# A two-layer DiT block on one Trainium2 core: two modulation parts moved out of the first stage, two rows computed during routing

## The chip, the cores and the metric

One core of a Trainium2 chip. The time is that of one execution on the device in microseconds (us), the median of several runs. The engines are PE (TensorE, matmuls; PEld is its loading of stationary operands), DVE (VectorE), ACT (ScalarE), POOL (GpSimd) and SP (SyncE, which here only issues transfers).

## What is computed

```python
for layer in range(2):                                   # x 1024x1024, ctx 256x1024, all f32
    sh1, sc1, gt1, sh2, sc2, gt2 = split(silu(c) @ w_mod[layer] + b_mod[layer], 6)
    csh1, csc1 = the same from c_ctx, for layer 0's hc = rmsnorm(ctx) * (1 + csc1) + csh1
    hx = rmsnorm(x, norm_mix_g[layer]) * (1 + sc1) + sh1
    yx = mixer_ab(hx, hc) if layer == 0 else mixer_chunk_gmlp(hx)
    x = x + gt1 * yx
    h = rmsnorm(x, norm_ffn_g[layer]) * (1 + sc2) + sh2
    aff = softmax(h @ w_router); gate, idx = top_k(aff.T, 128)      # 16 experts, 128 rows each
    xe = h[idx]
    ye = ((silu(xe @ w_gate) * (xe @ w_up)) @ w_down) * gate
    x = x + gt2 * scatter_add(ye, idx)
return rmsnorm(x, final_norm_g)
```

`mixer_ab` (layer 0) is a bidirectional mLSTM of 4 heads beside a window attention of 8 heads, both with the context; `mixer_chunk_gmlp` (layer 1) a gated MLP in chunks of 128 rows.

## The kernel before

Each modulation vector is a *part* (layer, w), w from 0 to 5 in the order sh1, sc1, gt1, sh2, sc2, gt2: 1024 columns of `w_mod`, 4 MB. PE computes a part in eight steps `mod_step` (line 661), one for each 128 rows of `w_mod`, of four matmuls each, in four column groups of the array, with `silu(c)` stationary. The stationary operand is 32 columns wide; it comes from `silw`, a tile of copies of `silu(c)` and `silu(c_ctx)` that is built once and lies in the pool `mcol` of layer 0.

Large products are made of three: weights and activations are split in two (`mh` + `ml`, `xH` + `xL`, both fp32r), ACT making the high part, DVE (POOL for some) the low one, and PE multiplies high by high, high by low and low by high.

The stages, in order:

- **First stage** (`start`). `start_mod` computes parts (0,0) and (0,1) for x and ctx, with 8 MB that SP loads. Then `heads_context` goes through the four mLSTM heads of the context: each loads two `w_in` tiles of 512 KB (ring `wraw`, two buffers, line 78 issues on SP), splits them (lines 70 and 71) and projects (line 302); between them it takes pieces of two generators, `rows()`, which normalises and transposes x, and `mods`, the parts (0,2) and (0,3) by `mod_part` (line 682), whose 16 tiles of 512 KB POOL loads (line 688) into the buffers of x rows.
- **Mixer of layer 0** (`layer0_a`, `layer0_b`). A generator of modulation parts, (0,4), (0,5), (1,0), (1,1), (1,2) and (1,5), gives one step between every few pieces of the attention (line 617). A row of kind gt1 or gt2 is written to DRAM (`s_gt`), since it is later read along the free axis by all partitions; the others are turned to columns in `modc`. `layer0_b` ends with row stores `s_x`, `s_xr`, and loads by `hole_load` (line 703) the parts (1,3) and (1,4) into eight tiles of the experts' ring (`moe_tile`, 1 MB each, line 709, on SP).
- **Routing of layer 0.** `hole_mods` (line 712) multiplies these two parts while DVE sorts. The sort (lines 1030 to 1071) finds each expert's 128 rows, PE transposes (lines 1057 to 1101) thresholds, totals and lists, and POOL gathers the rows of expert 0 by an indirect transfer (`fetch(0)`). The first weights (`moe_open`) are split meanwhile (line 1161).
- **Experts** (`experts`). For each: gathered rows transposed (`xe`), high and low parts `xH`, `xL`; 24 tiles of weights split on ACT (`mh`) and DVE (`ml`); products `g`, `u` and `d` on PE (line 1175), `sg` the gated activation, `xe<-d` the scaling by gate and gt2 row, a scatter by POOL. Of the ring, tiles of the numbers in `HELD` are issued by POOL behind the first gather, all others by SP, each as soon as its buffer is free. The gt2 row is read from `s_gt` at the start.
- **Layer 1**: `mixer_chunk_gmlp`, its routing, its experts in the same way; its routing has no modulation work.

A scheduler orders each engine's instructions at build time from the order in the code and from its own estimate of times; where it interleaves the loops differently the code does not show it.

Of the kernel before, what the change touches and what calls it, by code (L numbers as in the profile page):

```python
# [8 lines left out]
F32 = mybir.dt.float32  # L9
# [3 lines left out]
AF = mybir.ActivationFunctionType  # L13
ALU = mybir.AluOpType
# [7 lines left out]
KD = 8  # L22
# [16 lines left out]
class Kernel:  # L39
# [142 lines left out]
    def start(self, rings):  # L182
        nc, I = self.nc, self.I
        with ExitStack() as late:
# [32 lines left out]
            pm = self.pool(late, "pmod0", space=PSUM)  # L217
            mods = itertools.chain(*(self.mod_part(xp, "xt", sm, pm, pt, 0, w) for w in (2, 3)))
            self.heads_context(late, pt, Ws, rows(), mods)

    def heads_context(self, s, pt, Ws, more, mods):
# [15 lines left out]
        for hd in range(4):  # L237
            W = Ws.pop(0) if Ws else self.w_in(512 + hd * 128)
            acc = self.pa.tile([128, 512], F32, tag="acc", name="acc")
            self.proj(acc[:, :NCTX], W, hc, 0, NCTX)  # L240
            pad = cpool.tile([128, NCTX + 4], F32, tag="cpad", name="cpad")
            nc.vector.memset(pad[:, 0:2], 0.0)
            nc.vector.memset(pad[:, NCTX + 2:NCTX + 4], 0.0)
            nc.scalar.activation(pad[:, 2:2 + NCTX], acc[:, :NCTX], AF.Copy)
            kc = cpool.tile([128, NCTX], F32, tag="kcT", name="kcT")
            self.conv_silu(pad, NCTX, 4 + hd, kc)
            list(itertools.islice(more, 2))
            list(itertools.islice(mods, (1, 1, 3, 3)[hd]))
            W = Ws.pop(0) if Ws else self.w_in(1024 + hd * 128)
            acc = self.pa.tile([128, 512], F32, tag="acc", name="acc")  # L250
            self.proj(acc[:, :NCTX], W, hc, 0, NCTX)
            vc = cpool.tile([128, NCTX], F32, tag="vcT", name="vcT")
            nc.scalar.activation(vc, acc[:, :NCTX], AF.Copy)
            if kept:
                store(*kept)
            kept = hd, kc, vc
            list(itertools.islice(more, 2))
            list(itertools.islice(mods, (0, 2, 3, 3)[hd]))
        store(*kept)
        for _ in itertools.chain(more, mods):  # L260
            pass
# [292 lines left out]
    def layer0_a(self, rings):  # L554
        nc, I = self.nc, self.I
        with ExitStack() as s:
# [60 lines left out]
            mods = itertools.chain(*(self.mod_part(lm, "wm", lm, pa, pt, i // 6, i % 6) for i in range(4, 12) if (i // 6, i % 6) not in self.HOLE))  # L617
# [44 lines left out]
    def mod_step(self, acc, k, wm):  # L662

        for j in range(4):
            self.nc.tensor.matmul(acc[32 * j:32 * j + 32, :], self.silw[:, k].rearrange("p a s -> p (a s)"), wm[:, 256 * j:256 * (j + 1)],  # L665
                                  start=(k == 0), stop=(k == KD - 1))
# [36 lines left out]
    def hole_load(self):  # L703

        self.hole = []
        for layer, w in self.HOLE:
            for kp in range(4):
                raw = self.moe_tile()
                self.nc.sync.dma_start(out=raw, in_=self.I["w_mod"][layer, 256 * kp:256 * (kp + 1), D * w:D * (w + 1)].rearrange("(k p) c -> p k c", p=128))
                self.hole.append(raw)  # L710

    def hole_mods(self, p, ps, pt):

        for i, (layer, w) in enumerate(self.HOLE):
# [7 lines left out]
            self.nc.gpsimd.tensor_tensor(m, m, self.bcols[:, 48 * layer + 8 * w:48 * layer + 8 * w + 8], op=ALU.add)  # L722

# [125 lines left out]
    def layer0_b(self, l0):  # L849
# [8 lines left out]
        with ExitStack() as s:  # L858
# [44 lines left out]
            self.hole_load()  # L903
# [273 lines left out]
    def experts(self, layer):  # L1177
        nc, I = self.nc, self.I
        with ExitStack() as s:
# [7 lines left out]
            nc.scalar.dma_start(out=gt2, in_=row_ap(self.s_gt, (2 * layer + 1) * D, D))  # L1187
# [177 lines left out]
            with self.tc.issue_after(self.listed):  # L1365
                self.first = [self.moe_low(*w) for w in self.first]
            gather(0)
            self.lists(p, pp, layer, groups.pop(0))
            fetch(1)
            self.lists(p, pp, layer, groups.pop(0))  # L1370
# [233 lines left out]
    def run(self):  # L1604
        nc = self.nc
        with ExitStack() as es:
# [52 lines left out]
            self.moe_open(self.m0, 0, 5)  # L1659
            with ExitStack() as r:  # L1660
# [13 lines left out]
            with ExitStack() as l1:  # L1674
# [7 lines left out]
                self.moe_open(self.m1, 1, 11)  # L1682
                self.moe_rings(self.m1, 1)
# [60 lines left out]
```

## Time and profile before

| | |
|---|---|
| median of 3 runs | 2697.33 us (2695.96 to 2702.22) |
| the profiled execution | 2693.89 us, span 2692.1 us |
| mean granted clock of PE | 0.967 of full speed |
| busy PE / PEld / DVE | 2495.9 / 1972.3 / 1891.8 us |
| busy ACT / POOL | 1508.6 / 610.6 us |
| transfers | 643.70 MB, mean 239 GB/s |
| first stage | 0 to 120 us |
| routing of layer 0 | 787 to 829 us |
| experts of layer 0, first `g` product | from 829.28 us |
| routing of layer 1 | 2050 to 2085 us |
| experts of layer 1, first `g` product | from 2084.75 us |

Busy times are of the profiled execution, and engines work side by side, so they do not add up to the span. Times in the rows below are us from the start of that span.

### The profile page before, as it was taken

Reading aid. Unit: us, or ns where it says so; the run is one execution under the profiler, and the core shown is the slowest. Engines: PE = TensorE matmul, PEld = TensorE weight load, DVE = VectorE, ACT = ScalarE, POOL = GpSimd, SP = SyncE. Lnnn points to the kernel's source line nnn. Section 1 sums busy time; section 2 is a strip of 40 time slices with the busy share of each in tenths; the row PEclk is TensorE's granted clock in tenths of the full one; section 3 lists DMA queues with packets and bytes.
Section 4 is the critical chain, followed back from the end, with each engine's and each line's share of the span. In section 5 each row is a group of like instructions: output and inputs, shape, how many; then the busy total and the mean of one; then the engine's idle time right before and its main releaser. Section 6 shows DMA issues by size and latency. Waiting matters only on the chain.

```text
span 2692.1 us, 34493 instructions
## 1 busy us (share of the span) xinstructions
PE 2495.9 (93%) x12543; PEld 1972.3 (73%) x12543; DVE 1891.8 (70%) x2826; ACT 1508.6 (56%) x2262; POOL 610.6 (23%) x399
## 2 busy tenths in 40 slices
PE   5899999978987999999998999999994999999996
PEld 3667777767765888887776887888883788888774
DVE  4568768668548999998884373216405899999887
ACT  4345444444245888887864233322323888888774
POOL 0100100035401122121003434443451022221101
PEclk8899999999988999999999999999996999999998
DMA  8543434284369999999956323342326999999995
GB/s 293 181 110 112 128 122 139 90 278 154 134 237 350 373 387 392 387 379 368 361 166 194 86 75 117 128 136 71 126 77 228 373 373 387 380 379 385 357 364 186
DMA packets 241223, 643.70 MB, mean 239 GB/s; under 512 B 18257, under 2 KB 84989, under 8 KB 240029
## 3 DMA queue, kind: packets, MB, share of 16 engines
q1 hardware_dynamic: 206768, 536.81, 53.4%
q0 software_dynamic: 23792, 83.43, 10.9%
q10 hardware_dynamic: 10492, 21.26, 2.4%
q8 instruction: 98, 1.61, 0.2%
q14 instruction: 73, 0.59, 0.1%
HBM read 588.79 MB, written 50.02 MB: 237 GB/s over the span
## 4 chain that ended last, share of the span: by engine, by line
PE 78%; DVE 9%; issue 4%; DMA 4%; ACT 3%; POOL 1%; POOLq 0%; ACTq 0%; DVEq 0%; SPq 0%
PE g L1175 13%; PE u L1175 13%; PE d L1175 12%; PE acc L302 7%; PE acc L1485 7%; PE acc L1559 6%; PE acc L1507 6%; PE acc L841 2%; PE S L495 1%; DMA wm<-in_w_mod_dram 1%; DMA wraw<-in_ab_w_in_dram 1%; PE acc L665 1%; PE tr L1205 1%; PE tr L1249 1%; DVE s2k L1501 1%
## 5 line engine op out<-in xcount | busy, mean ns | idle before, releaser
L71 DVE TENSOR_TENSOR ml<-mraw,mh 128x1024 fp32r<-128x1024 f32 x750 | 874.6, 1222 | 62.1 <-ACT mh L70 61.6
L70 ACT ACTIVATE mh<-mraw 128x1024 fp32r<-128x1024 f32 x750 | 767.1, 1063 | 129.7 <-PE g L1175 62.6
L71 POOL TENSOR_TENSOR wl<-wraw,wh 128x1024 fp32r<-128x1024 f32 (+1 forms) x132 | 257.2, 1958 | 346.7 <-ACT wh L70 346.7
L70 ACT ACTIVATE wh<-wraw 128x1024 fp32r<-128x1024 f32 (+1 forms) x163 | 143.1, 893 | 323.8 <-issue 123.6
L1175 PE MATMUL g<-mh,xH 128*128 128x512 f32 x512 | 206.2, 403 | 1.4 <-ACT xH L1210 1.4
L1175 PE MATMUL g<-ml,xH 128*128 128x512 f32 x512 | 205.7, 402 | 1.9 <-DVE ml L71 1.9
L1193 POOL DMA_INDIRECT xe<-s_xr,idx x32 | 148.3, 4634 | 256.4 <-ACT mh L70 125.7
L1175 PE MATMUL g<-mh,xL 128*128 128x512 f32 x512 | 204.3, 399 | 0.0
L1175 PE MATMUL u<-ml,xH 128*128 128x512 f32 x512 | 203.7, 398 | 0.2
L1175 PE MATMUL d<-ml,hidH 128*128 128x512 f32 x496 | 197.6, 398 | 5.9 <-DVE ml L71 5.9
L1175 PE MATMUL u<-mh,xH 128*128 128x512 f32 x512 | 202.2, 395 | 0.0
L1175 PE MATMUL u<-mh,xL 128*128 128x512 f32 x512 | 202.2, 395 | 0.0
L1273 POOL DMA_INDIRECT s_x<-xe,idx x28 | 45.1, 1612 | 683.0 <-ACT hidH L1251 446.8
L1175 PE MATMUL d<-mh,hidH 128*128 128x512 f32 x496 | 198.1, 399 | 1.6 <-DVE o L1270 1.6
L1175 PE MATMUL d<-mh,hidL 128*128 128x512 f32 x496 | 196.3, 396 | 0.0
L1485 PE MATMUL acc<-wh,h2k 128*128 128x512 f32 x512 | 163.7, 400 | 1.2 <-DVE h2k L1467 1.2
L1507 PE MATMUL acc<-h2k,wh 128*128 128x512 f32 x512 | 160.2, 394 | 0.0
L302 PE MATMUL acc<-hH,wh 128*128 128x512 f32 (+1 forms) x368 | 150.3, 409 | 3.2 <-ACT hx L533 1.2
L1559 PE MATMUL acc<-wh,s2k 128*128 128x512 f32 x480 | 152.1, 397 | 0.0
L302 PE MATMUL acc<-hH,wl 128*128 128x512 f32 (+1 forms) x368 | 145.1, 394 | 0.0
L302 PE MATMUL acc<-hL,wh 128*128 128x512 f32 (+1 forms) x368 | 145.0, 394 | 0.0
L688 POOL DMA_DIRECT2D wm<-in_w_mod_dram x64 | 34.6, 543 | 442.3 <-PE acc L665 388.9
(474 smaller groups left out, 5182.5 us busy)
## 6 DMA issues: line engine op xcount, KB each, us to landing
mraw<-in_moe_w_down_dram SPq DMA_DIRECT2D x128, 1024.0 KB
mraw<-in_moe_w_gate_dram SPq DMA_DIRECT2D x125, 1024.0 KB
mraw<-in_moe_w_up_dram SPq DMA_DIRECT2D x123, 1024.0 KB
wm<-in_w_mod_dram POOLq DMA_DIRECT2D x64, 512.0 KB, 4.5
wraw<-in_gm_w_in_dram SPq DMA_DIRECT2D x64, 512.0 KB
wraw<-in_gm_w_out_dram SPq DMA_DIRECT2D x32, 512.0 KB
wraw<-in_ab_w_in_dram SPq DMA_DIRECT2D x30, 512.0 KB
wm<-in_w_mod_dram SPq DMA_DIRECT2D x8, 1024.0 KB
```

Of the source, the lines that this page charges most:

```text
L70: nc.scalar.activation(h, src, AF.Copy)
L71: i = (nc.gpsimd if eng == "pool" else nc.vector).tensor_tensor(l, src, h.bitcast(F32), op=ALU.subtract)
L302: nc.tensor.matmul(acc, a[:, k, :], b[:, k, c0:c0 + n], start=(k == 0 and i == 0), stop=(k == KD - 1 and i == 2))
L495: nc.tensor.transpose(S[i][:, 512 - nl + j * 128:640 - nl + j * 128], P[:, j * 128:(j + 1) * 128], self.ident)
L688: nc.gpsimd.dma_start(out=wm, in_=self.I["w_mod"][layer, k * 128:(k + 1) * 128, D * w:D * (w + 1)])
L841: nc.tensor.matmul(acc, a[:, k, t * 128:(t + 1) * 128], b[:, k % 2, :], start=(k == 0 and i == 0), stop=(k == 3 and i == 2))
L1175: nc.tensor.matmul(acc[:, sl], a[:, k, :], b[:, sl], start=(k == 0 and i == 0), stop=(k == KD - 1 and i == 2))
L1193: f = nc.gpsimd.indirect_dma_start(out=xe, out_offset=None, in_=self.s_xr[layer], in_offset=bass.IndirectOffsetOnAxis(ap=self.idx[e], axis=0))
L1273: nc.gpsimd.indirect_dma_start(out=self.s_x[layer], out_offset=bass.IndirectOffsetOnAxis(ap=self.idx[e], axis=0), in_=o, in_offset=None, c ...
L1485: nc.tensor.matmul(acc[t], a[k][:, ts], b[:, k2, :], start=(k == 0 and i == 0), stop=(k == KD - 1 and i == 2))
L1507: nc.tensor.matmul(acc, a[:, k, :], b[k], start=(k == 0 and i == 0), stop=(k == KD - 1 and i == 2))
L1559: nc.tensor.matmul(acc, a[:, ts], b[k2], start=(c == 0 and i == 0), stop=(c == 15 and i == 2))
```

## The change

- Parts (0,2) and (0,3) are no longer in the first stage but in the generator of layer 0's mixer; the gate rows of the experts' outputs, parts (0,5) and (1,5), leave that generator.
- Each gate row is now computed in `experts`, by the new `hole_gate`, right after `fetch(0)` and ahead of `gather(0)` in the code. Its weights are four ring tiles: for layer 0 two loaded at the end of `hole_load`, two behind the first five weight tiles of `moe_open`; for layer 1 four behind `moe_open`. The accumulator is a `d` tile of PSUM, the bias comes by an ACT transfer, POOL adds it, ACT issues the write to `s_gt`. The read of the row moves behind `fetch(1)`.
- `mod_step` takes as its stationary operand one column of `sil`, read 32 times (stride 0), in place of the copies in `silw`.
- As the ring holds four more tiles of `w_mod` in each layer (12 in place of 8 before layer 0's experts), the numbers in `HELD` now meet other weight tiles.

```diff
     def start(self, rings):
...
-            pm = self.pool(late, "pmod0", space=PSUM)
-            mods = itertools.chain(*(self.mod_part(xp, "xt", sm, pm, pt, 0, w) for w in (2, 3)))
-            self.heads_context(late, pt, Ws, rows(), mods)
+            self.heads_context(late, pt, Ws, rows())
-    def heads_context(self, s, pt, Ws, more, mods):
+    def heads_context(self, s, pt, Ws, more):
-            list(itertools.islice(mods, (1, 1, 3, 3)[hd]))
...
-            list(itertools.islice(mods, (0, 2, 3, 3)[hd]))
...
...
-            mods = itertools.chain(*(self.mod_part(lm, "wm", lm, pa, pt, i // 6, i % 6) for i in range(4, 12) if (i // 6, i % 6) not in self.HOLE))
+            mods = itertools.chain(*(self.mod_part(lm, "wm", lm, pa, pt, i // 6, i % 6) for i in (2, 3, 4, 6, 7, 8)))
     def mod_step(self, acc, k, wm):
-            self.nc.tensor.matmul(acc[32 * j:32 * j + 32, :], self.silw[:, k].rearrange("p a s -> p (a s)"), wm[:, 256 * j:256 * (j + 1)],
+            self.nc.tensor.matmul(acc[32 * j:32 * j + 32, :], self.sil[:, k:k + 1].to_broadcast([128, 32]), wm[:, 256 * j:256 * (j + 1)],
...
+    def hole_gate(self, p, pd, layer):
+        nc, b = self.nc, self.I["b_mod"]
+        t = p.tile([128, D], F32, tag="sg", name="mrows")
+        rows, bias = t[:, 0:256], t[:, 256:512]
+        nc.scalar.dma_start(out=bias, in_=bass.AP(tensor=b.tensor, offset=b.offset + D * (6 * layer + 5), ap=[[256, 4], [0, 32], [1, 256]]))
+        acc = pd.tile([128, D], F32, tag="d", name="d")[:, 0:256]
+        for k in range(KD):
+            self.mod_step(acc, k, self.hole[k // 2][:, k % 2, :])
+        self.hole = []
+        nc.scalar.activation(rows, acc, AF.Copy)
+        nc.gpsimd.tensor_tensor(rows, rows, bias, op=ALU.add)
+        nc.scalar.dma_start(out=self.s_gt[2 * layer + 1].rearrange("(j c) -> j c", j=4), in_=rows[0:128:32, :])
...
-            self.hole_load()
+            self.hole = []
+            self.hole_load(self.HOLE)
+            self.hole_load([(0, 5)], range(2))
...
-            nc.scalar.dma_start(out=gt2, in_=row_ap(self.s_gt, (2 * layer + 1) * D, D))
...
             fetch(0)
...
+            self.hole_gate(p, pd, layer)
             gather(0)
             self.lists(p, pp, layer, groups.pop(0))
             fetch(1)
+            nc.scalar.dma_start(out=gt2, in_=row_ap(self.s_gt, (2 * layer + 1) * D, D))
...
             self.moe_open(self.m0, 0, 5)
+            self.hole_load([(0, 5)], range(2, 4))
...
                 self.moe_open(self.m1, 1, 11)
+                self.hole_load([(1, 5)])
```

How the built programs' instructions stand, at three places. First, DVE at the start of layer 0's sort, with what each instruction waits for (`work` is the sort's input, `sort` its result), before and then with the change:

```order
L1013 COPY rows<-tr 128x128 [waits PE_49]
L1014 COPY work<-rows 128x128 [waits DVE_49]
L1030 MAX sort_7116<-work 128x8 [waits DMASW3_49,DMASW1_49,DMASW5_49,DVE_49,PE_49]
L1030 MAX sort_7116<-work 128x8
L1033 MATCH_REPLACE work<-sort_7116,work 128x64 [waits DVE_49] x2
```
```order
L1025 COPY rows<-tr 128x128 [waits PE_49]
L1026 COPY work<-rows 128x128 [waits DVE_49]
L1042 MAX sort_7012<-work 128x8 [waits DMASW5_49,DMASW7_49,DMASW1_49,DVE_49]
L1042 MAX sort_7012<-work 128x8
L1045 MATCH_REPLACE work<-sort_7012,work 128x64 [waits DVE_49] x2
```
The first `MAX` has lost its wait on PE. On PE, at the same place, the routing transposes `tr` follow the two modulation parts `mod`, before and then with the change (`d<-mraw,sil` is the gate row):

```order
L665 MATMUL mod<-mraw,silw 32x256 x64
L677 MATMUL tr<-cst,mrows 128x128 x4
L1094 LDWEIGHTS zerob
L1094 MATMUL tr<-zerob 128x32
L1057 MATMUL tr<-sort_7115,cst 16x128
L1062 MATMUL tr<-thr,cst 128x1
L1076 MATMUL tr<-tot,cst 128x2
L1077 MATMUL tr<-tot,cst 128x2
L1085 MATMUL tr<-cst,gt 128x128
```
```order
L661 MATMUL mod<-mraw,sil 32x256 x29
L673 MATMUL tr<-cst,mrows 128x128 x2
L1106 LDWEIGHTS zerob
L1106 MATMUL tr<-zerob 128x32
L661 MATMUL d<-mraw,sil 32x256 x16
L1069 MATMUL tr<-sort_7011,cst 16x128
L1074 MATMUL tr<-thr,cst 128x1
L661 MATMUL d<-mraw,sil 32x256 x5
L1088 MATMUL tr<-tot,cst 128x2
L1089 MATMUL tr<-tot,cst 128x2
L661 MATMUL d<-mraw,sil 32x256 x3
L1097 MATMUL tr<-cst,gt 128x128
L661 MATMUL d<-mraw,sil 32x256 x5
```
The gate row's 32 matmuls go ahead of and between the routing transposes; the last of them stand behind the transposes of `gt` and of the lists, ahead of those of `xe`. Second, ACT from the splits of the first weights (`mh`, lines 1161 and 1173) to the first expert, before and then with the change:

```order
L1161 ACTIVATE mh<-mraw 128x1024 x4
L719 ACTIVATE mrows<-mod 128x256 x2
L720 ACTIVATE modc<-tr 128x8 x2
L1161 ACTIVATE mh<-mraw 128x1024
L1187 DMA gt_7328<-s_gt 128x1024
L1207 ACTIVATE xe<-tr,modc,gs_6484 128x128 x5
L1210 ACTIVATE xH<-xe 128x512
L1207 ACTIVATE xe<-tr,modc,gs_6484 128x128 x3
L1210 ACTIVATE xH<-xe 128x512
L70 ACTIVATE mh<-mraw 128x1024 x8
```
```order
L712 DMA mrows<-in_b_mod_dram 128x1x256
L717 ACTIVATE mrows<-d 128x256
L1173 ACTIVATE mh<-mraw 128x1024 x2
L719 DMA s_gt<-mrows 4x256
L1218 ACTIVATE xe<-tr,modc,gs_6376 128x128
L1173 ACTIVATE mh<-mraw 128x1024 x2
L1218 ACTIVATE xe<-tr,modc,gs_6376 128x128 x4
L1173 ACTIVATE mh<-mraw 128x1024
L1221 ACTIVATE xH<-xe 128x512
L1218 ACTIVATE xe<-tr,modc,gs_6376 128x128 x3
L1382 DMA gt_7224<-s_gt 128x1024
L1221 ACTIVATE xH<-xe 128x512
L70 ACTIVATE mh<-mraw 128x1024 x8
```
Five splits that stood ahead of the modulation copies and of the gather's evictions `xe` now stand behind the gate row's copy, three of them between the evictions. Third, DVE in layer 1 after `sg` of expert 10, up to the next `sg`, before and then with the change:

```order
L1230 TENSOR_TENSOR sg<-u,sg 128x512 x2
L71 TENSOR_TENSOR ml<-mraw,mh 128x1024
L1211 TENSOR_TENSOR xL<-xe,xH 128x512
L71 TENSOR_TENSOR ml<-mraw,mh 128x1024
L1211 TENSOR_TENSOR xL<-xe,xH 128x512
L71 TENSOR_TENSOR ml<-mraw,mh 128x1024 x5
L1270 SCALAR_TENSOR_TENSOR xe<-d,gate,gt_17208 128x512 x2
L71 TENSOR_TENSOR ml<-mraw,mh 128x1024
L1252 TENSOR_TENSOR hidL<-tr,hidH 128x512 x2
L71 TENSOR_TENSOR ml<-mraw,mh 128x1024 x14
```
```order
L1241 TENSOR_TENSOR sg<-u,sg 128x512 x2
L1222 TENSOR_TENSOR xL<-xe,xH 128x512 x2
L71 TENSOR_TENSOR ml<-mraw,mh 128x1024 x9
L1281 SCALAR_TENSOR_TENSOR xe<-d,gate,gt_17150 128x512 x2
L1263 TENSOR_TENSOR hidL<-tr,hidH 128x512 x2
L71 TENSOR_TENSOR ml<-mraw,mh 128x1024 x15
```
The two `xL`, which stood apart among the splits `ml`, stand together ahead of nine splits.

## Rows read from the trace of the kernel before

**Rows 1.** The page, part 4: shares of the chain that ended last, by engine.

```profile
PE 78%; DVE 9%; issue 4%; DMA 4%; ACT 3%; POOL 1%; POOLq 0%; ACTq 0%; DVEq 0%; SPq 0%
```

**Rows 2.** Windows, first stage: us, busy by engine (records), PEclk, DMA share, GB/s.

```profile
20.00:40.00 20.00, 11.91 (x78) 3.32 (x71) 5.17 (x13) 1.06 (x1) 1.10 (x2) 0.78 0.97 332
40.00:60.00 20.00, 15.39 (x96) 11.87 (x94) 15.95 (x43) 18.24 (x37) 1.13 (x2) 0.80 0.81 276
...
80.00:100.00 20.00, 17.50 (x152) 13.51 (x146) 14.01 (x25) 8.50 (x13) 4.14 (x7) 1.00 0.88 255
...
140.00:160.00 20.00, 20.00 (x89) 16.06 (x88) 13.46 (x13) 9.92 (x12) 0.00 (x0) 1.00 0.26 62
```

**Rows 3.** Chain of waits, 20 to 125 us: start, length, what was waited for.

```profile
26.05 10.84 DMA wm<-in_w_mod_dram
...
61.08 6.00 DMA wraw<-in_ab_w_in_dram
...
75.34 8.96 DMA wraw<-in_ab_w_in_dram
...
89.33 8.97 DMA wraw<-in_ab_w_in_dram
...
100.67 3.04 DMA wraw<-in_ab_w_in_dram
...
109.05 10.50 PE acc L302 x72
```

**Rows 4.** Line 688 up to 100 us: modulation loads issued by POOL, ns, first, last.

```profile
L688 POOL DMA_DIRECT2D wm<-in_w_mod_dram x16: 527/529/715, 24.3 to 93.6; - x16
...
DMA to landing us min/median/max: 4.1/6.7/11.6
```

**Rows 5.** Line 665, whole kernel: weight loads and matmuls of modulation, ns min/median/max.

```profile
L665 PEld LDWEIGHTS acc<-wm,silw x512: 106/109/153, 54.9 to 516.0; 128*32 128x32 f32 x171
L665 PE MATMUL acc<-wm,silw x512: 379/379/635, 54.9 to 516.2; 128*32 128x256 f32 x171
```

**Rows 6.** Timeline of DVE, layer 0's sort: start, busy, what [idle before <-releaser].

```profile
797.21 0.35 DVE L1030 MAX8 sort<-work 128x8 f32<-128x64 f32 x2 [8.69 <-PE mod L665]
```

**Rows 7.** Chain of waits, layer 0's routing, 784 to 835 us.

```profile
812.75 0.60 PE tr L1062 x2
...
817.34 0.46 PE tr L1085
...
820.48 5.18 DMA xe<-s_xr,idx
```

**Rows 8.** Timeline of ACT, layer 0's routing, 786 to 803 us.

```profile
790.58 3.88 ACT L1161 ACTIVATE mh<-mraw 128x1024 fp32r<-128x1024 f32 x4
...
801.95 1.06 ACT L1161 ACTIVATE mh<-mraw 128x1024 fp32r<-128x1024 f32 x1 [3.66 <-DMA mraw<-in_moe_w_gate_dram]
```

**Rows 9.** Windows, routing of layer 0 and (last row) layer 1.

```profile
788.00:792.00 4.00, 4.00 (x40) 1.83 (x40) 0.48 (x2) 4.00 (x5) 0.22 (x1) 0.50 0.92 368
...
797.00:805.00 8.00, 1.11 (x9) 0.47 (x5) 7.55 (x60) 1.74 (x4) 2.55 (x6) 0.85 1.01 404
...
820.00:826.00 6.00, 0.29 (x2) 0.29 (x3) 5.97 (x10) 0.00 (x0) 4.02 (x4) 0.50 0.53 176
...
2070.00:2080.00 10.00, 1.43 (x12) 1.00 (x12) 8.06 (x16) 0.00 (x0) 2.62 (x2) 0.50 1.02 397
```

**Rows 10.** Chain of waits, layer 1's routing: the first expert's gather.

```profile
2075.19 5.94 DMA xe<-s_xr,idx
```

**Rows 11.** Windows, layer 0: from one expert's first down product `d` to the next.

```profile
1167.66:1203.01 35.35, 35.35 (x164) 28.66 (x162) 34.45 (x35) 29.70 (x38) 5.74 (x2) 1.00 1.03 392
1203.01:1241.32 38.31, 38.31 (x180) 31.01 (x178) 32.80 (x35) 31.49 (x46) 4.61 (x2) 1.00 1.02 384
...
1280.02:1317.18 37.16, 36.18 (x160) 28.44 (x160) 32.70 (x33) 29.24 (x38) 2.74 (x2) 1.00 1.00 365
```

**Rows 12.** Waits, 1280.02 to 1317.18 us: us in total, times, longest.

```profile
PE d L1175 <- DVE ml L71: 1.0, 1, 1.0
```

More of the change, by code (lines that the diff above doesn't have):

```diff
@@ L257, in heads_context @@
             list(itertools.islice(more, 2))
-            list(itertools.islice(mods, (0, 2, 3, 3)[hd]))
         store(*kept)
-        for _ in itertools.chain(more, mods):
+        for _ in more:
             pass
@@ L701, with hole_load @@
     HOLE = ((1, 3), (1, 4))
[L703 to L707, printed above, removed]
+    def hole_load(self, parts, kps=range(4)):
+        for layer, w in parts:
+            for kp in kps:
                 raw = self.moe_tile()
@@ L722, in hole_mods @@
             self.nc.gpsimd.tensor_tensor(m, m, self.bcols[:, 48 * layer + 8 * w:48 * layer + 8 * w + 8], op=ALU.add)
+        del self.hole[:4 * len(self.HOLE)]
     def lstm_main(self, lp, hd):
```

## The prediction

> **What bounds the kernel now.** I read the page first: PE holds 78% of the chain that ended last, DVE 9%, DMA 4% [rows 1]. An edit pays only where that chain leaves PE, so I looked for those places. The change touches three: the first stage, and the two routing stretches between a layer's mixer and its experts. It also reaches the expert loops, where PE is nearly always busy but not in every expert.
>
> In the first stage the windows by stretch show PE at 15.4 and 17.5 of 20 us, DVE at 16.0 and 14.0, and DMA engines 0.81 and 0.88 busy; at 140 us PE has no idle time left and DMA is at 0.26 [rows 2]. The chain of the stage says what is late: after the wait for the modulation weights it hangs three times on a `w_in` load, for 6.00, 8.96 and 8.97 us, and its last PE block, 72 matmuls for the context, starts at 109.05 us [rows 3].
>
> **Part 1, two modulation parts leave the first stage.** Parts (0,2) and (0,3) go to the later mixer stage. With them go 16 loads of 512 KB that POOL issued between 24.3 and 93.6 us, each landing after 4.1 to 11.6 us [rows 4]: 8.4 MB out of a stage that moves 255 to 276 GB/s [rows 2], some 30 us of DMA time. Two of these are queued beside the weights that start the stage; 1 MB at the 332 GB/s of that stretch [rows 2] is 3 us, taken off the 10.84 us wait [rows 3]. What is late next is compute. DVE works 16.0 us in 40 to 60, 14.0 in 80 to 100 [rows 2], some 15 between them and, at the last pace, 6 more to 109: 51 us. If DVE never waited from 37 us on, the last block would start at 88 (21 us sooner); if it idled as it does from 40 to 60 us, 4 of 20, where no long DMA wait stands in the chain, at 37 + 51 / 0.8 = 101 (8 us sooner). A second way gives the same middle: the three waits and the last of 3.04 us are 27 us, and the last, of 64 KB, met little traffic and cost 3.04 [rows 3]; four such are 12, so 15 go, and with the 3 ahead 18. I take 16 us, the ends being 8 and 21. The rows of the changed order of DVE and ACT here are other ones, but the same work.
>
> Does the mixer stage take the two parts for nothing? It has six parts before and six after, since (0,5) and (1,5) leave it: the same steps between the same attention pieces. Its weight loads change place, not number. So the 16 us are carried to its end, where PE is the limit [rows 2]. The matmuls' stationary operand becomes one column read 32 times, where it was a tile of copies. A weight load of this kind takes 109 ns and lies under a matmul of 379 ns [rows 5]: nothing if it stays, and if it doubled, still beneath the matmul. Zero, both ways.
>
> **Part 2, layer 0's routing.** DVE has its sort's input at 788.5 us and idles 8.69 us, until PE has done the two late parts of modulation, because the sort's tiles lie where the copied operand was [rows 6]. Of the first order pieces the one of before has the wait on PE, the other hasn't: the sort can start at 788.5 us. That takes 8.69 us from a chain that runs on through sort, lists and the gather (5.18 us) to the first expert [rows 7]. Given back: the new order of ACT puts three of the first weight splits between the gather's evictions (the second order pieces). A split of this sort takes 3.88 / 4 = 0.97 us in a row and 1.06 us alone [rows 8]: 3.1 us. The gate's matmuls also stand in PE's queue between the routing transposes, and half of them wait there for two tiles that SP requests as second and third behind the row stores. Before, the second load behind those stores was a weight tile, which ACT had at 801.95 us [rows 8]; so the two land at about 802 and, 1 MB at 404 GB/s [rows 9] later, 804.6. The transposes they stand behind are those of 812.75 and 817.34 [rows 7], moved up by 8.7 to 804.1 and 808.7. In time, so nothing; at worst the wait eats the whole gain, and DVE, ACT and POOL, which follow those transposes, wait with it.
>
> The gather of the first expert now falls in a time of full DMA. At a share of 0.53 it took 5.18 us, in layer 1, where the share was 1.02 just before, 5.94 [rows 7, 9, 10]: 0.8 us more. The Trainium skill ("DMA: Bandwidth & Descriptors", section "Issuing engines are not separate DMA queues") says that transfers of all issuing engines share the same 16 engines and interleave; those two rows agree. By it the gate's weights, now on SP's queue, still delay POOL's gather; if queues were separate the sum would be 0.8 lower. Sum: 8.7 - 3.1 - 0.8 = **4.8 us gained**, between 0 and 8.7.
>
> **Part 3, layer 1's routing.** Here nothing is taken away: 32 matmuls (each two records in the trace), four 1 MB loads, one ACT copy, one POOL add, a bias load, a 4 KB write and the later read of the gate row are added. PE idles for most of this stretch (1.43 busy of 10 us at 2070, clock 0.50) [rows 9]. At that clock, the lower of its two levels (1.2 of 2.4 GHz), 40 such records took 4.00 us [rows 9], the 16 of a tile take 1.6. They fill PE's idle time, but the one or two pieces that stand just ahead of a routing transpose may cost 1 to 2 us; the last piece lies inside the gather's 5.94 us [rows 10]. The 4.2 MB go ahead of expert weights while DMA is full (397 GB/s [rows 9]): 10.6 us of it. The ring already runs ahead of the first expert, so I take 2 us for all of it; ends 0 and 10.6. The gate row's write and read must end before the first output is scaled, a whole expert later: no cost.
>
> **Part 4, the experts' order.** The diff does not show it, the order of DVE does: the loop has two orders. In one the two `xL` of the next expert stand apart, with splits between them; in the other both stand ahead of nine splits. The last order pieces show the two, after expert 10 of layer 1. Counted through DVE's whole order, the second kind begins, in each layer, in part after the 12th expert's `sg` and fully after the 13th's; now, in layer 0, in part after the 9th's and fully after the 11th's, and in layer 1 after the 8th's at once. Its price is in the trace: an expert in the first order takes 35.35 us with PE always busy, in the second 37.16, PE idle for 0.98 us of it [rows 11], at `d`, until DVE's split `ml` comes [rows 12]. That is 1.81 us an expert. The expert at the turn, of both orders, takes 38.31 [rows 11], 3 us more than the first. Layer 0: two full ones, 3.6, and another of the turn's kind, 0 to 3, together 5 us; layer 1: five full ones, 9, less one of the turn, 3, together 6 us. **11 us lost**, between 0 and 15.
>
> Layer 0's mixer takes two 1 MB loads more ahead of its row stores, while DMA has room (a share of 0.26 in its first part [rows 2]); nothing.
>
> **Sum:** -16 - 4.8 + 2 + 11 = -7.8 us. The profiled execution took 2693.89 us (span 2692.1, 1.8 around it), so 2686.1 in its terms. It is 3.4 below the median of 2697.33, so I forecast **2689.5 us** for the median. A measurement of this kernel can tell about 0.2%, 5.4 us, from no change.
>
> **Rivals.**
> - *The later experts' order costs nothing*: the 1.81 us belongs to the last experts of a layer (fewer gathers, scatters ahead), not to the order. For it: the rows have the second order only there. Against: what PE waits for is an `ml` [rows 12], and where that stands the order sets. Then -18.8: 2678.5 us. Chance 0.17.
> - *The first stage isn't freed*: only two `w_in` tiles can be in flight, so each load starts late whatever the traffic, and the three waits stay; just the 3 us at the start go. For it: DMA is 0.81 busy there, not full [rows 2]. Against: loads of the same size take 4 to 12 us as traffic goes [rows 4]. Then -3 - 4.8 + 2 + 11 = +5.2: 2702.5. Chance 0.15, half of it slower.
> - *Slower: the gate's weights starve the first experts.* An expert needs 12 tiles of 1 MB, 12.6 MB in 35.35 us or 356 GB/s, and DMA is at a share of 1.00 to 1.03 with 365 to 392 [rows 11]: what is put ahead is made up slowly, over three experts or more, and till then it is missing from the ring: 10.6 us in layer 1 and, for 2.1 MB, 5.4 us in layer 0, 16 in place of 2. It decides as soon as a first-expert split waits for its tile longer than the ring is ahead. Then -16 - 4.8 + 16 + 11 = +6.2: 2703.5. Against: at the end of the second kind's expert PE waits for a split's subtraction [rows 12], not for a tile. Chance 0.12, two thirds of it slower. The Trainium skill ("DMA: Bandwidth & Descriptors", section "Where 436 GB/s comes from") puts a core's limit from HBM at about 358 GB/s; by it nothing would ever be made up and 2703.5 would be the time, but the rows' 392 lies above it.
> - *The sort waits on*, for its other releasers or for PE in another place, so part 2 gains nothing and keeps its 3.9: -16 + 3.9 + 2 + 11 = +0.9: 2698.2. Chance 0.08, no difference.
>
> **The numbers.** The forecast's own case has 0.48: with the ends of the first stage and of the order it reaches from 2681 to 2697, 0.34 of it faster by over 0.2% and 0.14 within. With the rivals: faster 0.34 + 0.17 = 0.51; the same 0.14 + 0.07 + 0.04 + 0.08 = 0.33; slower 0.08 + 0.08 = 0.16. The range 2675 to 2703 takes in all of these but their outer ends and half of the slower rival; the likeliest case alone is 2681 to 2697.
>
> **What would show it.** Right: the last context block starts near 93 us, with the `w_in` waits of the chain under 5 us; DVE's first sort instruction stands with no idle time before it; the first `g` of layer 0 comes some 21 us earlier in all; `d` to `d` is 37.2 us from about the ninth expert on. Wrong: the context block at 105 or later; an idle PE at the gate's matmuls for a `w_mod` tile over 3 us; `ml` or `mh` waiting for an expert's tile in the first two experts; or 35.4 us an expert under the second order.

## The result

The changed kernel takes 2713.3 us (median of 4 runs, 2710.31 to 2715.96) against 2697.46 us before: a ratio of 1.0055, 95% interval 1.0043 to 1.0067. It is slower by 15.8 us where 7.8 us less were forecast. The profiled execution took 2711.22 us, its span is 2709.4. The page's parts 1 and 4 (busy time; shares of the chain), to be held against [rows 1]:

```profile
PE 2513.1 (93%) x12543; PEld 1979.0 (73%) x12543; DVE 1893.3 (70%) x2824; ACT 1504.2 (56%) x2264; POOL 564.3 (21%) x381
...
PE 76%; DVE 8%; DMA 6%; issue 5%; ACT 3%; POOL 1%; POOLq 0%; ACTq 0%; SPq 0%; DVEq 0%
```
PE's share of the chain falls from 78 to 76% and DMA's rises from 4 to 6%: two new waits for transfers stand in it. One, of 29.60 us in layer 0, is followed up below. The other, of 15.71 us ahead of layer 1's gather (2067.41 us), costs nothing to speak of: the gather's row numbers (`idx`) are ready only 0.1 us before it ends. Where the time went is seen by following the same events through both timelines (us from the span's start):

| event | before | after | forecast shift | shift |
|---|---|---|---|---|
| last context block of the first stage | 109.05 | 93.22 | -16 | -15.8 |
| last projection of layer 0's mixer (line 302, now 298) | 556.6 | 541.3 | -16 | -15.3 |
| routing of layer 0, first transpose (line 1010, now 1022) | 787.5 | 773.6 | -16 | -13.9 |
| first gather issued | 820.48 | 799.26 | -24.7 | -21.2 |
| first `g` of layer 0 | 829.28 | 813.54 | -20.8 | -15.7 |
| first `g` of expert 2 | 894.57 | 892.22 | -20.8 | -2.4 |
| first `g` of expert 15 | 1363.79 | 1369.90 | -16 | +6.1 |
| first `g` of layer 1 | 2084.75 | 2092.84 | -14 | +8.1 |
| first `g` of expert 2, layer 1 | 2150.32 | 2160.85 | -14 | +10.5 |
| first `g` of expert 15, layer 1 | 2620.18 | 2637.96 | -8 | +17.8 |

The first stage, windows by stretch (columns as in [rows 2]) and chain:

```profile
40.00:60.00 20.00, 16.65 (x108) 14.59 (x109) 16.79 (x41) 19.11 (x40) 0.00 (x0) 0.88 0.61 199
...
80.00:100.00 20.00, 14.17 (x94) 12.86 (x93) 16.29 (x33) 11.55 (x21) 0.34 (x2) 0.74 0.37 103
```
```profile
24.27 9.41 DMA wm<-in_w_mod_dram
...
77.10 3.79 DMA wraw<-in_ab_w_in_dram
...
93.22 9.72 PE acc L298 x72
```
DMA is at 0.61 and 0.37 where it was at 0.81 and 0.88; of the three long `w_in` waits [rows 3] one of 3.79 us is left. At the sort, DVE's timeline has 0.30 us of idleness in the place of 8.69 [rows 6]:

```profile
774.96 0.35 DVE L1042 MAX8 sort<-work 128x8 f32<-128x64 f32 x2 [0.30 <-DVE work L1026]
```
Then the gain goes. The chain of waits around the first gather of layer 0 (its times are start and length):

```profile
799.26 7.83 DMA xe<-s_xr,idx
...
813.54 0.80 PE g L1187
...
821.27 29.60 DMA mraw<-in_moe_w_gate_dram
```
The gather takes 7.83 us where it took 5.18 [rows 7], and right after the first `g` a load of the second expert's gate tile stands in the chain for 29.60 us. ACT's timeline shows who waits for it and for the two tiles ahead of it, their splits:

```profile
840.73 2.00 ACT L70 ACTIVATE mh<-mraw 128x1024 fp32r<-128x1024 f32 x2 [5.84 <-PE tr L1216]
845.85 2.00 ACT L70 ACTIVATE mh<-mraw 128x1024 fp32r<-128x1024 f32 x2 [3.11 <-DMA mraw<-in_moe_w_gate_dram]
850.97 1.06 ACT L70 ACTIVATE mh<-mraw 128x1024 fp32r<-128x1024 f32 x1 [3.12 <-DMA mraw<-in_moe_w_gate_dram]
```
The first of these waits is put down to PE, whose transposes `tr` end at the same time; but the first gate tile, issued at 819.86 us, lands 20.8 us later, at 840.6. In ACT's order the evictions `xe` of this expert's rows stand behind these splits, and PE stands still until they come:

```profile
853.48 1.12 PE L1260 MATMUL tr<-cst,sg 128*128 128x128 f32 x4 [12.84 <-ACT xe L1218]
```
These are tiles that POOL issues behind the first gather. The loads at that line of the changed kernel (x count: ns of issue, first and last issue), and then of the kernel before:

```profile
L1156 POOL DMA_DIRECT2D mraw<-in_moe_w_gate_dram x3: 720/728/732, 819.9 to 821.3; - x3
L1156 POOL DMA_DIRECT2D mraw<-in_moe_w_up_dram x2: 757/764/772, 814.6 to 815.3; - x2
...
DMA to landing us min/median/max: 13.1/20.8/29.6
```
```profile
L1144 POOL DMA_DIRECT2D mraw<-in_moe_w_up_dram x3: 703/762/772, 824.2 to 838.4; - x3
L1144 POOL DMA_DIRECT2D mraw<-in_moe_w_gate_dram x2: 711/728/746, 822.8 to 823.5; - x2
...
DMA to landing us min/median/max: 5.9/9.5/11.4
```
Before, the five tiles were gate tiles 2 and 3 and up tiles 0 to 2 of expert 1 (the second, as they are numbered from 0); now they are up tiles 2 and 3 of expert 0 and gate tiles 0 to 2 of expert 1, which are needed sooner and land later, 20.8 us after their issue in the median against 9.5. First to second `g` takes 40.81 us in the place of 28.22: 12.6 us.

From expert 9 on the late order shows (windows between the first `g` of experts 9, 10, 11 and of 13, 14, columns as in [rows 11]):

```profile
1141.63:1182.00 40.37, 38.65 (x186) 30.39 (x185) 36.22 (x39) 29.47 (x37) 9.75 (x2) 0.96 0.94 340
1182.00:1220.27 38.27, 36.54 (x162) 28.54 (x161) 33.66 (x33) 29.14 (x37) 3.45 (x2) 1.00 0.94 349
...
1295.55:1332.72 37.17, 36.19 (x161) 28.45 (x160) 32.71 (x32) 29.26 (x37) 2.57 (x2) 1.00 1.00 370
```

### The profile page after: what moved, and what is told of

It is laid out like the page before. It is cut to its first block, busy times and chain, and to the rows that moved or that the text cites. A ratio compares the mean times of both kernels' runs of the same rounds, so it can differ in the third digit from the quotient of the medians.

```text
span 2709.4 us, 34455 instructions
## 1 busy us (share of the span) xinstructions
PE 2513.1 (93%) x12543; PEld 1979.0 (73%) x12543; DVE 1893.3 (70%) x2824; ACT 1504.2 (56%) x2264; POOL 564.3 (21%) x381
## 3 DMA queue, kind: packets, MB, share of 16 engines
q1 hardware_dynamic: 208944, 545.20, 54.0%
q0 software_dynamic: 21136, 74.77, 9.7%
## 4 chain that ended last, share of the span: by engine, by line
PE 76%; DVE 8%; DMA 6%; issue 5%; ACT 3%; POOL 1%; POOLq 0%; ACTq 0%; SPq 0%; DVEq 0%
PE g L1187 13%; PE u L1187 12%; PE d L1187 12%; PE acc L298 7%; PE acc L1498 7%; PE acc L1572 6%; PE acc L1520 6%; PE acc L851 2%; PE S L491 1%; DMA wm<-in_w_mod_dram 1%; DVE ml L71 1%; DMA mraw<-in_moe_w_gate_dram 1%; PE acc L661 1%; DVE s2k L1514 1%; PE tr L1216 1%
## 5 line engine op out<-in xcount | busy, mean ns | idle before, releaser
L1204 POOL DMA_INDIRECT xe<-s_xr,idx x32 | 112.4, 3512 | 296.3 <-ACT mh L70 109.2
L1187 PEld LDWEIGHTS g<-ml,xH 128*128 128x128 f32 x512 | 97.8, 191 | 31.3 <-DVE ml L71 8.9
```

The source lines that it names most:

```text
L1187: nc.tensor.matmul(acc[:, sl], a[:, k, :], b[:, sl], start=(k == 0 and i == 0), stop=(k == KD - 1 and i == 2))
L1204: f = nc.gpsimd.indirect_dma_start(out=xe, out_offset=None, in_=self.s_xr[layer], in_offset=bass.IndirectOffsetOnAxis(ap=self.idx[e], axis=0))
```

## The experiments

Each ran with the kernel before on the same chip; ratios are to it, with 95% intervals. e1 to e4, e5 to e8 and e9 to e12 each share a chip and the runs of the kernel before (medians 2697.11, 2698.42 and 2697.96 us). Where something is read from a timeline, it is from one profiled execution, and medians of a kernel lie up to 6 us from it.

**e1: the numbers of the late-issued tiles follow the tiles.**

```diff
-    HELD = ((18, 23), (11, 14))
+    HELD = ((22, 27), (15, 18))
```

> The changed kernel with the numbers of the late-issued tiles moved up by four in each layer, so that POOL again issues the same weight tiles behind the first gather as before the change; nothing else. Theory A (the shifted numbers): the second expert's first gate tiles were among them, landed 29.6 us after their issue, and PE lost 12.6 us between the first and the second expert of layer 0 and 2.5 us in layer 1. Those come back: first to second g of layer 0 falls from 40.8 to about 28 us, total about 2713 - 15 = 2698 us. Theory B (the bytes: 2 MB and 4 MB of modulation weights put ahead are missing from the ring, whoever issues the others): the g to g stays near 40 us and the total near 2713. The later experts of both layers should be as in the changed kernel under both (8.5 and 7.2 us lost).

Measured 2699.75 us (ratio 1.0011, 1.0000 to 1.0022), 13.6 below the changed kernel. First to second `g` falls from 40.81 to 29.50 us. The late experts are as in the changed kernel, but for one of layer 0 (38.8 us at a granted clock of 1.00 in the place of 40.4 at 0.96). Theory A: with the modulation weights still ahead, 1.3 us are left of the 12.6. In layer 1, where 2.5 us were expected back, nothing changes: first to third `g` is 68.0 us in both. The loads that POOL issues now:

```profile
L1156 POOL DMA_DIRECT2D mraw<-in_moe_w_up_dram x3: 715/748/752, 800.5 to 819.5; - x3
...
L1156 POOL DMA_DIRECT2D mraw<-in_moe_w_gate_dram x2: 767/770/772, 818.0 to 818.8; - x2
...
DMA to landing us min/median/max: 9.9/16.0/20.4
```
They still take up to 20.4 us to land, but the tiles are those needed later, and nothing waits for them.

**e2: the gate rows back in the mixer**, which then has eight parts, one step in four fill steps; the first stage stays free.

```diff
-            mods = itertools.chain(*(self.mod_part(lm, "wm", lm, pa, pt, i // 6, i % 6) for i in (2, 3, 4, 6, 7, 8)))
+            mods = itertools.chain(*(self.mod_part(lm, "wm", lm, pa, pt, i // 6, i % 6) for i in (2, 3, 4, 5, 6, 7, 8, 11)))
...
-                    if next(steps) % 5 == 4:
+                    if next(steps) % 4 == 3:
...
-            self.hole_gate(p, pd, layer)
+            if layer not in (0, 1):
+                self.hole_gate(p, pd, layer)
```

> The changed kernel without its gate rows in the routing: parts (0,5) and (1,5) are computed in layer 0's mixer beside (0,2) and (0,3), one step in every four pieces in place of five; the first stage stays free of modulation and the stationary operand is the column. Theory A (each gain is real, the losses all hang on the gate rows in the routing): last context block at 93 us as in the changed kernel, layer 0's routing shorter by 7 to 8.7 us, mixer a little longer (0 to 4 us, 16 more PE blocks of 0.4 us), no loss in the experts beyond 1 us: 2697.5 - 16 - 8 + 3 = about 2677 us. Theory B (the first stage's gain is given back later, in the mixer or as a wait for weights): 2690 us or more.

Measured 2694.37 us (0.9987, 0.9975 to 0.9999): theory B. The gain of the first stage is given back in the mixer: the last context block starts at 92.34 us, the mixer's last projection at 558.3, later than before.

**e8: the reverse**, e1 with the first stage as before and four parts in the mixer, (0,4), (1,0), (1,1), (1,2).

> The kernel of e1 with the first stage as before the change: parts (0,2) and (0,3) are computed there again, and the mixer's generator has the four parts (0,4), (1,0), (1,1), (1,2). Theory A (a part costs about 8 us wherever it is put, in the first stage by its load, in the mixer by PE and by waits for its load, as e2 has it): the last context block is back at 109 us, the mixer ends no more than 3 us from e1, total 2697 to 2702 us. Theory B (the mixer takes parts for nothing): the 16 us of the first stage are lost, 2714 to 2717 us.

Measured 2706.31 us (1.0029, 1.0019 to 1.0038), 6.6 over e1, or some 5 when each is held against its own runs of the kernel before: between the two, nearer to A. The mixer's projections, first to last start (third field), in the kernel before, the changed one, e2 and e8:

```profile
L302 PE MATMUL acc<-hH,wh x368: 387/392/505, 119.4 to 556.6; 128*128 128x512 f32 x176, 128*16 128x512 f32 x8
```
```profile
L298 PE MATMUL acc<-hH,wh x368: 387/389/504, 102.8 to 541.3; 128*128 128x512 f32 x176, 128*16 128x512 f32 x8
```
```profile
L298 PE MATMUL acc<-hH,wh x368: 387/393/797, 102.7 to 558.3; 128*128 128x512 f32 x176, 128*16 128x512 f32 x8
```
```profile
L302 PE MATMUL acc<-hH,wh x368: 387/389/628, 119.1 to 545.2; 128*128 128x512 f32 x176, 128*16 128x512 f32 x8
```
From first to last start these are 437.2, 438.5, 455.6 and 426.1 us, with 6, 6, 8 and 4 parts. A part costs (437.2 - 426.1) / 2 = 5.6 to (455.6 - 438.5) / 2 = 8.6 us in the mixer; in the first stage the two together cost (109.05 - 93.22) / 2 = 7.9 each. So a part moved from the one to the other earns little: two of them are worth 3.5 us at the mixer's end (545.2 in e8, 541.7 in e1). The change earned most of its 16 us because two other parts left the mixer for the routing.

**e3: the column alone**, the kernel before with the one edit in `mod_step` (the line in the diff above).

> The kernel before with one edit: the stationary operand of modulation is the column itself. The sort loses its wait on PE; ACT's order in the routing changes little (two copies apart), and the experts' order has the turn one expert later in layer 0. Theory A: the sort starts 8.7 us sooner and nothing is given back, 2697.5 - 8.7 = about 2689 us, with d to d as before. Theory B (the sort then waits for another releaser, or the gather for the rows' stores): 0 to 3 us gained, 2694 to 2697.

Measured 2694.20 us (0.9988, 0.9976 to 1.0001), 2.9 below, which is hardly clear of none. The time is that of theory B, but its reason isn't: the sort starts at once:

```profile
793.87 0.35 DVE L1030 MAX8 sort<-work 128x8 f32<-128x64 f32 x2
```
From the routing's first transpose to the first gather it takes 25.8 us (792.8 to 818.58) where it took 33.0: 7.2 gained, of 8.7. But that transpose itself comes 5.3 us later than before: 1.2 of it stand at the mixer's last projection (557.8 us), and from there to the transpose it takes 235.0 us where it took 230.9. The work of this stretch is the same in all kernels of this study, and it takes 230 to 235 us in them. Why it is long in this one stays open.

**e4, e5: the expert loop's order held.** Both stand on e1. e4 ties the two `xL` to the first two splits of the down weights. e5 writes five down splits ahead of the scaling of `sg`, and ties the evictions `xm` behind the high part that ACT split last (e4 does this too):

```diff
-                    nc.scalar.activation(xm[:, k, :], trs[k // 4][:, k % 4 * 128:k % 4 * 128 + 128], AF.Identity, bias=self.sh2[:, k:k + 1], scale=self.gs2[:, k:k + 1])
+                    with self.tc.issue_after(self.last_hi.ins) if e > 2 else ExitStack():
+                        nc.scalar.activation(xm[:, k, :], trs[k // 4][:, k % 4 * 128:k % 4 * 128 + 128], AF.Identity, bias=self.sh2[:, k:k + 1], scale=self.gs2[:, k:k + 1])
...
+                if e > 1:
+                    self.first = [self.moe_w("moe_w_down", layer, e - 1, k) for k in range(5)]
                 for b in range(2):
                     sl = slice(512 * b, 512 * (b + 1))
-                    nc.vector.tensor_tensor(sg[:, sl], u[:, sl], sg[:, sl], op=ALU.mult)
+                    with self.tc.issue_after(self.last_split.ins) if e > 1 else ExitStack():
+                        nc.vector.tensor_tensor(sg[:, sl], u[:, sl], sg[:, sl], op=ALU.mult)
```

> The first kernel of this set with the order of the expert loop held in place: from the third expert on, the two xL subtractions are written behind the first and the second split of the down weights, and the xe evictions behind the last split of the up weights. No work is added or left out. Theory A (the order costs the time): the late experts take 35.4 to 36.2 us in place of 37.2 and 38 to 40, some 10 to 13 of the 15.7 us that the two loops lost come back, and with them part of what the kernel before loses in its own last experts: 12 to 20 us below the first kernel of this set, 2678 to 2686. Theory B (the last experts are slow by their place, whatever the order): same time as the first kernel of this set.

> The kernel of e1 with another way of holding the expert loop's order: from the third expert on, five splits of the down weights are written ahead of the scaling of sg, which is ordered behind them on DVE, and the xe evictions behind them on ACT. All experts of a layer then have the order of the early ones (sg, xL, ml, xL, ml). No work is added or left out. e4 did not do this: it moved the xL subtractions but left only three down splits ahead of sg. Theory A (what costs is the number of down splits that DVE has done when PE ends u; three in the late order, five in the early one): every expert takes 35.4 to 36.2 us, the 27.8 us that e1 has over that from its 8th expert on in both layers come back, 2700 - 28 = about 2672 us; at least 15 of them. Theory B (the last experts are slow by their place): d to d stays at 37.2 there and the total near 2700 us.

e4 is slower: 2717.18 us (1.0083, 1.0065 to 1.0100). Its late experts take 38.76 us, PE idle for 1.7 of them, where e1 has 37.2:

```profile
1327.00:1365.76 38.76, 37.03 (x161) 28.28 (x160) 32.52 (x32) 29.59 (x37) 1.59 (x1) 1.00 0.92 339
```
So the order sets the time, but `xL` is not the part of it that does. e5 takes 2679.40 us (0.9931, 0.9916 to 0.9946), 20.3 below e1, theory A by its lower bound (15); 28 were expected. In e5, e6 and e7 the last two experts of layer 1 multiply some of their down rows by other tiles of expert 14 and 15, as many products, and three more tiles are loaded; **e9** leaves these experts in their old place:

> The kernel of e5 with the down splits of layer 1's expert 14 left in their old place, since the tiles of the last two experts are listed anew there. Theory A: as e5, 2679 us or up to 2 us more, d to d 35.4 us in all late experts but two. Theory B (e5 was short because it took other tiles there): 2690 or more.

Measured 2678.90 us (0.9933, 0.9917 to 0.9949). Expert 13 of both layers, in e9:

```profile
1278.71:1314.05 35.34, 35.34 (x161) 28.66 (x160) 32.79 (x32) 30.05 (x37) 7.23 (x2) 1.00 1.02 379
...
2538.29:2573.65 35.36, 35.36 (x161) 28.68 (x160) 32.79 (x32) 30.06 (x37) 5.95 (x2) 1.00 1.00 372
```
PE has no idle time, 35.35 us in the place of 37.2. One expert in each layer still takes 39.4 us; there the list work, which the early experts spread over two, stands in one, and the granted clock is 0.96 where it is 1.00 in expert 13.

**e6 and e12: the same order in the kernel before**, e12 with the two experts left as in e9.

> The kernel before with the same ordering of the expert loop as e5. Theory A: its last four experts of each layer lose their 10 us, 2697 - 20 = about 2677 us. Theory B: 2697 us.

> The kernel before with the expert loop's order held as in e9. Theory A: as e6, 2685 us; the changed kernel with its tiles' numbers and its order mended (e9) is then faster than this by 4 to 8 us, which is what the change itself is worth. Theory B (with the order mended the change is worth nothing): e9 and this agree within 2 us.

e6 takes 2685.10 us (0.9950, 0.9937 to 0.9964), e12 2683.88 us (0.9952, 0.9936 to 0.9969): 13 to 14 less than before, not 20. In the timelines the late experts give back some 6 us a layer, not 10, and the first two lose 1.8 to 2.4, the second of them at a clock of 0.96. That makes some 8 us; what the medians have beyond it these two traces do not show. e9 is 5.0 us below e12, theory A at its lower end, but the two intervals overlap: what the change is worth with the order held is not clear of noise.

**e10: the kernel before, POOL issuing the tiles that it issues in the changed kernel**, `HELD = ((14, 19), (7, 10))`, no modulation weights more.

> The kernel before with the numbers of the late-issued tiles moved down by four, so that POOL issues the tiles that it issues in the changed kernel (the last two up tiles of expert 0 and the first three gate tiles of expert 1), with no modulation weights added. In the built order the late kind of the expert loop begins five experts sooner in layer 0 and two sooner in layer 1. Theory A (the tiles cost what they cost because full DMA delays them behind later tiles; before, SP's ring is already full when POOL issues them): first to second g of layer 0 stays within 4 us of 28.2; the order alone adds 5 x 1.8 = 9 us in layer 0 and 3 to 4 in layer 1: 2697 + 13 = about 2710 us. Theory B (these tiles by themselves cost 12 us whoever else loads): first to second g near 40 us, 2720 us or more. Theory C (order costs nothing without the gate rows): 2697 to 2701.

Measured 2709.76 us (1.0049, 1.0034 to 1.0064): theory A to the microsecond. First to second `g` takes 29.09 us; the same tiles land sooner than in the changed kernel:

```profile
L1144 POOL DMA_DIRECT2D mraw<-in_moe_w_gate_dram x3: 703/771/775, 825.2 to 839.1; - x3
L1144 POOL DMA_DIRECT2D mraw<-in_moe_w_up_dram x2: 702/729/756, 823.8 to 824.5; - x2
...
DMA to landing us min/median/max: 6.9/8.7/11.6
```
The time went in the later experts, in the late kind from expert 8 on, without any gate row in the program (expert 10, between its first `g` and the next):

```profile
1188.43:1225.62 37.19, 36.20 (x161) 28.45 (x160) 32.70 (x32) 29.25 (x37) 2.81 (x2) 1.00 1.00 376
```
From the first `g` of expert 7 to that of expert 15 it is 298.5 us against 290.9 before; in layer 1 3.2 us more. The 12.6 us of the changed kernel thus need both, the near tiles issued late and loads of SP beside them (the last section shows these); the late order needs neither gate rows nor their weights.

**e7: two splits ahead of the gather** in the place of five, on e5 (`range(2 if layer == 0 else 5)` at line 1020 of the changed kernel), so that ACT has none between the evictions.

> The kernel of e5 with two in place of five weight splits written ahead of the first gather of layer 0, so that ACT has no split between the evictions of the gathered rows. Theory A (three splits of 1.06 us lie in the chain from the gather to the first product): the first g of layer 0 comes 3 us sooner after the gather, and the total is 2 to 3 us below e5. Theory B (the first g waits for its weights or for DVE anyway): no difference from e5 over 1 us.

Measured 2683.66 us (0.9943, 0.9931 to 0.9956), 4.3 over e5. From the gather's issue to the first `g` it takes 11.4 us (801.68 to 813.12) against 14.3: the 2.9 us of theory A. But first to second `g` takes 36.59 us against 29.47; what was saved ahead of the first product is lost behind it, and more. There PE waits 5.30 us for the second expert's gathered rows (at 825.18 us).

**e11: e9 with no tile issued late**, `HELD = ((0, 0), (0, 0))`.

> The kernel of e9 with no tile issued late: SP issues every weight tile in the order of use. Theory A (the order of landing is what matters in the first expert): first to second g stays at 29 to 30 us, the gather of the first expert takes longer, as SP's loads are all in front of it, 8 to 12 us; total 2679 to 2685 us. Theory B (late issue is needed to let the gather through): gather over 12 us, total 2690 or more.

Measured 2679.19 us (0.9928, 0.9913 to 0.9944): as e9, and the gather takes 7.98 us in layer 0. With the order kept, issuing tiles late earns nothing.

## Why the prediction was wrong

**Part 1** held: -16 forecast, -15.8 at the last context block and -15.3 at the mixer's end. Its reason for carrying it, six parts before and after, was the right one; e2 and e8 show how much hung on it. That the operand read with stride 0 costs nothing held too: in the mixer its matmuls take 379 ns and its weight loads 108, as before (379 and 109).

**Part 2** was 4.8 us gained; at the first `g` it is -15.7 + 13.9 = 1.8 gained, from the routing's first transpose on. The sort gave 7.4 of the 8.7 (33.03 to 25.67 us up to the gather): besides the 0.30 us, DVE waits 0.72 in the middle of it (at 785.87 us) for a column that the late parts still have to give. The splits between the evictions cost what was said (2.9 in e7, 3.1 forecast). The gather was mis-sized: 2.65 us more, forecast 0.8. The gate's matmuls did not wait for their tiles.

**The step that failed** is the next one, for which there was no term: the change's description says that the numbers in `HELD` now meet other weight tiles, and the sum put nothing for it. Five 1 MB tiles needed one to two products later were issued behind the gather, while SP's loads of later tiles took half of the DMA engines' time. The cost is 12.6 us in layer 0, of which e1 gets back 11.3 by the numbers alone. The rival *the gate's weights starve the first experts* came near to the time by luck. What it named as a sign, `mh` waiting for an expert's tile in the first two experts, is what the profile shows, but it put 10.6 of its 16 us in layer 1, where some 4 are lost up to the third `g`, and 5.4 in layer 0. And its mechanism was another: with the same bytes and the right tiles (e1) 1.3 us are left, and with those tiles and without the bytes (e10) 0.9.

**Part 4** had the mechanism and a size too small: 11 us forecast, (6.1 + 2.4) + (17.8 - 10.5) = 15.8 measured, between the `g` of expert 2 and of expert 15. A full late expert costs 37.17 us as read before. The turn was mis-sized: in layer 0 40.37 and 38.27 us, in layer 1 37.00 and 39.12. In the longest of each layer DVE does three steps of list work (`oh`), in the early experts at most two, and PE waits 1.2 us and more for them and for the splits behind them; in layer 0 its clock is 0.96 besides, and e1 takes 38.8 there at 1.00. The rival *the later experts' order costs nothing* falls by e9 (same places, 35.35 us) and e10 (other places, 37.19). That PE waits there for an `ml` was right: in e10 too it is idle for 0.98 us at `d` for one. But where the `xL` stand, by which the prediction told the two orders apart, is not what makes it wait: in e4 they stand apart, and its late experts take 38.8 us. The likeliest reason is the number of down splits done when `u` ends: from the first `g` of expert 13 on, 15 splits stand ahead of `sg` in the changed kernel, 14 in e4 and 19 in e9. But e4 and e9 differ in more than that.

**Part 3**, 2 us at the start of layer 1, measured 2.0 at the first `g`, but by luck: 1.5 of them are there at the routing's first transpose already (2050.39 before, 2057.96 us now), from layer 1's mixer, for which nothing was put, and the gate row's pieces cost 0.5. The gate's matmuls did wait for a tile, 5.8 us (line by line view: busy, mean ns | idle before):

```profile
L661 PE MATMUL d<-mraw,sil 128*32 128x256 f32 x128 | 16.9, 552 | 5.8 <-DMA mraw<-in_w_mod_dram 5.8
```
It lay beside the sort's work. Another 2.4 us went in the first two experts of layer 1, most of it with PE's clock. From the second `g` to the third, in the changed kernel and before:

```profile
2122.30:2160.85 38.55, 37.99 (x182) 30.50 (x182) 34.11 (x38) 31.67 (x41) 1.31 (x1) 0.96 1.03 409
```
```profile
2113.19:2150.32 37.13, 36.58 (x181) 29.44 (x182) 33.82 (x38) 31.54 (x41) 1.32 (x1) 1.00 0.95 363
```
PE is idle for 0.55 us in both, but the clock granted is 0.96 in the one and 1.00 in the other. In all kernels of this study this stretch takes 38.3 to 38.6 us at 0.96 and 37.1 to 37.2 at 1.00. e3 is among the former, and it has no gate row; PE idles for 1.4 us just ahead of it in e3 as in the kernel before. What lets the clock fall stays open.

In the profiled executions the change costs 17.3 us where -7.8 were forecast. These 25.1 are 2.1 ahead of layer 0's routing, 3.0 in it (part 2), 13.3 in the first two experts of layer 0, 2.4 in those of layer 1 and 4.8 in the later ones (part 4), less 0.5 behind the last.

## What to carry to other kernels

Where a ring of buffers gives tiles special treatment by their number, a change that puts other tiles into the ring changes who gets it: look the numbers up again and ask when each tile is needed, and which other loads run while it is on its way. A part of the work that is moved costs something where it arrives, even on an engine that looks busy with other things; measure the stage with one part more and one less. Where a scheduler orders the program, compare the built order of every loop, not only the edited places; here an order held by hand was worth 14 us before the change and 20 after, by the medians.

## What was not expected of the hardware

A load that POOL issues takes 5.9 to 11.4 us for 1 MB in the kernel before and 13.1 to 29.6 in the changed one, at the same width. Whether SP's loads run beside it makes the difference. The DMA queues while these tiles land, in the changed kernel from 822 to 851 us and in the kernel before from 823 to 836 (packets, MB, share of 16 engines; `q0` holds POOL's loads, `q1` SP's, since from before to after the one falls from 83.43 to 74.77 MB and the other rises from 536.81 to 545.20, as the loads of two parts go from POOL to SP):

```profile
q1 hardware_dynamic: 1663, 6.39, 54.8%
q0 software_dynamic: 1443, 5.51, 47.8%
```
```profile
q0 software_dynamic: 1095, 4.17, 90.2%
q1 hardware_dynamic: 10, 0.04, 3.9%
```
Before, the first three tiles have DMA almost to themselves. In the changed kernel each queue gets half, and POOL's tiles land one behind the other: the three gate tiles are split from 840.73, 845.85 and 850.97 us on, 5.1 us apart. No gate row is needed for that: in e3 POOL issues its last four tiles only at 836.6 to 838.8 us, beside SP's loads (`q1` 53.8%, `q0` 48.5% from 837 to 862 us), and they land late too:

```profile
DMA to landing us min/median/max: 6.1/15.5/24.3
```
They are the tiles that are needed later, and nothing waits for them. Why SP's loads go on at that time in the one kernel and not in the other was not isolated.

The Trainium skill ("DMA: Bandwidth & Descriptors", section "Issuing engines are not separate DMA queues") says that all issuers' transfers interleave on the same engines; the rows above agree, with 54.8% for the one queue and 47.8% for the other: a tile that is needed first gets no precedence from that.
